# Output projection split, its SSD half between the last GLA heads; layer 1's modulation as running sums on VectorE

## The chip, the core and the metric

The kernel runs on one core of one Trainium2 chip. Its time is device microseconds of one execution, from the first instruction to the end. TensorE (PE) multiplies, VectorE (DVE), ScalarE (ACT) and GpSimd (POOL) work elementwise, SyncE (SP) issues most of the DMAs. Every engine takes its own instructions in order. The order in which the instructions of an engine stand in its queue is laid down at compile time, by a planner that goes by the order of the program, by an estimate of every instruction's duration and by when buffers come free. So an instruction written earlier can stand later in the queue.

## What is computed

Two layers of a diffusion backbone over 256 latent tokens and 256 context tokens (512 columns in all, context first), width 1024. Each layer has a mixer and a squared-ReLU MLP, and every sub-layer is modulated by shift, scale and gate, which come from a matrix product with the conditioning vector (two streams: c for the latents, c_ctx for the context).

```python
for layer in range(DEPTH):
    need_ctx = layer < DEPTH - 1
    mod_l = (silu(c) @ ada_w[layer] + ada_b[layer])[:, None, :]
    mod_c = (silu(c_ctx) @ ada_w[layer] + ada_b[layer])[None, None, :]
    sh1l, sc1l, g1l, sh2l, sc2l, g2l = split(mod_l, 6)
    hl = modulate(rmsnorm(x, norm1_w[layer]), sh1l, sc1l)
    # layer 0: SSD heads || GLA heads;  layer 1: HGRN2 heads || S5 groups
    ol, oc = mixer(hl, hc, ...)          # concat([y, o]) @ w_out
    x = x + g1l * ol
    x = x + g2l * sq_relu_mlp(modulate(rmsnorm(x, norm2_w[layer]), sh2l, sc2l), w1, w2)
    if need_ctx:                         # the same for the context, layer 0 only
        ...
return rmsnorm(x, final_norm_w)
```

In layer 0 the output projection takes 2048 inputs, 1024 of the SSD heads (y) and 1024 of the GLA heads (o). In layer 1 the context's stream needs shift and scale of the first norm alone, since nothing of it is used after that mixer.

## The kernel before

**Products.** Activations lie with features on the 128 partitions and the 512 tokens along the free dimension. A product in float32 is made of three matmuls (`mm3`, all recorded at line 99): each operand is split into a rounded high half and the rest, and high x high, high x low and low x high are added up in PSUM. `wtile` (line 214 issues its DMA on SP's queue) loads 512 KB of weights, a raw tile of 128x1024; ACT copies it to the high half (`whi`, line 80) and DVE subtracts to get the low half (`wlo`, line 87). Raw tiles have four buffers (`RAW`), high and low halves four each (`HL`). A tile of one output block is 8 k-tiles x 3 = 24 matmuls of 512 columns.

**Modulation.** `ada_steps` works out one third of a layer's modulation, a group of 2048 of the 6144 columns. A step loads two raw tiles of 512 KB from ada_w (line 233, SP's queue, from the same four raw buffers) and multiplies them in PE (line 237) with `cs`, 32 columns of which two hold the conditioning of the two streams: four matmuls of 512 columns, each into its own 32 partitions of one PSUM tile. The trace records each as two, so a step has eight records. Eight such steps, then a copy on ACT, then four transposes and the bias: ten steps in all. `ad` runs groups 1 and 2 of layer 0 (group 1 holds gate 1 and shift 2); `step(ad, n)` takes n of its steps. Group (0, 1) is steps 1 to 10 and group (0, 2) is 11 to 20.

**The GLA heads.** Four pairs of heads, `t_` = 0 to 3. `gla_in(t_)` projects q and k out of `h` (tiles hhi and hlo), two output tiles of 24 matmuls, makes the gates and runs a chain of elementwise work between DVE and ACT (`lin_elem`) with short PE pieces (`lin_states`). `gla_out(t_)` makes the attention of both heads with matmuls of 64 and 128 columns, masks on DVE, and scales the result into `vtm`. The loop is a pipeline: the projections of the next pair are written ahead of `gla_out` of this one. `fill` is other work put between: `z_proj`, four groups of 256 columns (96 matmuls of 256 columns each) that gate the SSD result in `xtm`, and a fifth step that norms it. `ZN` says how many of its steps stand before each pair, `ADN` how many modulation steps.

**The output projection** comes after the last pair. It turns xtm (the SSD result, token on partition) with transposes into the two halves of a matmul operand, in the buffers hhi and hlo that h had; loads the residual stream `xT` (2 MB, ACT's queue, into the buffer of xtm, which has to have been read); and makes eight output tiles of the SSD half, each added into xT by `add_out` on DVE with gate 1. Then the GLA half: vtm is turned, four tiles with a modulation step before each, and the last four tiles by halves of the tokens, between which the next norm begins.

**The MLP of layer 0** multiplies 64 weight tiles. `up(k)` makes one hidden block and squares its ReLU (`relu2`: ACT, DVE, ACT, DVE); a second-layer tile is added into xT by `add_out` on DVE. After each of them `step(extra)` takes one step of `background()`, which goes to and fro between `s5_setup` (tables for layer 1, mostly POOL and small DVE instructions) and the modulation of layer 1, groups (1, 0), (1, 1) and (1, 2), 30 steps in all.

Of the kernel before, what the change touches and what calls it, by code (L numbers as in the profile page):

```python
# [10 lines left out]
F32R = mybir.dt.float32r  # L11
# [18 lines left out]
DTM = 11  # L30
NF = 4
AR = 12
ZN = 3, 1, 2, 2
ADN = 0, 6, 11, 0
WA = 0, 1
QP = -2, 1, 2, 5
VP = -2, -1, 0, -1
GP = -1, 0, 4, 6
# [3 lines left out]
def emit(tc, A, out):  # L42
# [43 lines left out]
    def tt(eng, o, a, b, op):  # L86
        eng.tensor_tensor(out=o, in0=a, in1=b, op=op)  # L87
# [7 lines left out]
    def stt(eng, o, a, s, b, op0, op1):  # L95
        eng.scalar_tensor_tensor(out=o, in0=a, scalar=s, in1=b, op0=op0, op1=op1)  # L96
# [47 lines left out]
    cs = tl(cp, [P, 8, 32], "cs")  # L144
    mod = [tl(cp, [P, 48, 2], f"mod{l}") for l in range(2)]
    dskip = tl(cp, [P, 16], "dskip")
    dtb = tl(cp, [64, 1], "dtb")
    nega = tl(cp, [64, 1], "nega")

# [77 lines left out]
    def ada_steps(l, g3, scratch):  # L227
        ps = ps_s()
        for k in range(8):
            raws = [tl(wp, [P, 1024], "wraw", bufs=RAW) for _ in range(2)]  # L230
            for hf in range(2):
                c0 = g3 * 2048 + 1024 * hf
                Q.dma_start(out=raws[hf], in_=A["ada_w"][l, k * P:(k + 1) * P, c0:c0 + 1024])

            last = None
            for gg in (3, 2, 1, 0):
                ins = PE.matmul(ps[32 * gg:32 * gg + 32], lhsT=cs[:, k], rhs=raws[gg // 2][:, gg % 2 * T:gg % 2 * T + T],  # L237
                                start=(k == 0), stop=(k == 7), skip_group_check=True, tile_position=(0, 32 * gg))
                if last is not None:
                    behind(ins, last)  # L240
                last = ins
            yield
        sb = scratch()
        act(sb, ps, AF.Copy)
        yield
        p2 = ps_s()
        for b in range(4):
            tr(p2[:, b * P:(b + 1) * P], sb[:, b * P:(b + 1) * P])
        src = p2.rearrange("p (b g r) -> p g b r", b=4, r=32)[:, :, :, 0:2]
        bias = vA[:, l * 48 + g3 * 16:l * 48 + g3 * 16 + 16].rearrange("p (g b) -> p g b", g=4)  # L250
        dst = mod[l][:, g3 * 16:g3 * 16 + 16].rearrange("p (g b) s -> p g b s", g=4)
        for s in range(2):
            tt(V, dst[:, :, :, s], src[:, :, :, s], bias, ADD)
        yield

    def ada_all(scratch, *lg):
# [3 lines left out]
    def step(it, n=1):  # L260
        for _ in range(n):
            next(it, None)

    def drain(it):
        for _ in it:
            pass
# [998 lines left out]
    def gla_w(t_):  # L1265
        return [wtile(W0, 0, 8, c0 + P * t_, P) for c0 in (3104, 3616)]

    def gla_in(t_, ws):
        qk = []
        for w, sc in zip(ws, (0.125, 1.0)):  # L1270
            ps = ps_d()
            gemm_f(ps, w, ktiles(h))
            d_ = tl(g2, [P, T], "gq" if sc != 1.0 else "gk", bufs=QB)
            act(d_, ps, AF.Copy, scale=sc)
            qk.append(d_)

        def chain(d):
            ps = ps_s()
            b0 = 64 + 32 * d
            mm(ps, gw[b0:b0 + 16, t_ * P:(t_ + 1) * P], dlr[b0:b0 + 16])  # L1280
            gb = vB[:, 24 + 4 * d + t_:25 + 4 * d + t_]
            e1 = tl(g2, [P, T], "ge1", bufs=2)
            act(e1, ps, AF.Abs, bias=gb)
            yield
            act(e1, e1, AF.Exp, scale=-1.0)
            yield
            act(e1, e1, AF.Ln, bias=1.0)
            lg = tl(g2, [P, T], "gc", bufs=2)
            ts(V, lg, ps, gb, ADD, 0.0, MIN)
            yield  # L1290
            tt(V, lg, lg, e1, SUB)
            yield
            nm = f"g{d}"
            qt, kt, kd, el, em = yield from lin_elem(g2, d, lg, qk[0], qk[1], None, 1.0 / 16.0, 0, nm)
            sts = yield from lin_states(g2, d, kd, el, em, lambda c, hh: vtm[:, c, (2 * t_ + hh) * P:(2 * t_ + hh + 1) * P],
                                        2, 0, nm)
            return qt, kt, sts

        return both([chain(d) for d in range(2)])
# [25 lines left out]
            lin_out(g2, pmask, units, put)  # L1325

    scr[0] = lambda: tl(g2, [P, T], "ge1", bufs=2)
    cur = gla_in(0, gla_w(0))
    wn = gla_w(1)
    for t_ in range(4):  # L1330
        step(fill, ZN[t_])
        nxt = gla_in(t_ + 1, wn) if t_ < 3 else None
        wn = gla_w(t_ + 2) if t_ < 2 else None
        step(ad, ADN[t_])
        if t_ == 3:
            drain(fill)
            step(ad, max(0, 10 - adn[0]))
        gla_out(t_, cur)
        cur = nxt
    gla.close()  # L1340


    lo_eng[:] = [V]
    WO = A["ssd_gla_w_out"][0]
    mgs = ExitStack()
    mg = pool("mixg", stack=mgs, side="right")
    scr[0] = lambda: tl(mg, [P, T], "adasb")
    for part, src in enumerate((xtm, vtm)):
        if part == 0:
            mx = [tl(hp, [P, 8, T], n, F32R) for n in ("hhi", "hlo")]  # L1350
        else:
            mx = [tl(mg, [P, 8, T], n, F32R) for n in ("mgh", "mgl")]
        for f in range(8):
            ps = ps_s()
            for c in range(4):
                tr(ps[:, c * P:(c + 1) * P], src[:, c, f * P:(f + 1) * P])
            nw = vB[:, 16 + f:17 + f] if part == 0 else vB[:, 96:97]
            act(mx[0][:, f], ps, AF.Copy, scale=nw)
            stt(V, mx[1][:, f], ps, nw, mx[0][:, f], MUL, SUB)
        if part == 0:  # L1360
            xT = tl(xp, [P, 8, T], "xtm")
            S.dma_start(out=xT, in_=xd.rearrange("k p t -> p k t"))
        def add_out(m):
            def put(s, ps):
                a = HALF[s]
                stt(V, xT[:, m, a], ps[:, a], mod[0][:, 16 + m, s:s + 1], xT[:, m, a], MUL, ADD)
            return put

        nf = 8 if part == 0 else 4
        for m in range(nf):  # L1370
            step(ad, WA[part])
            w = wtile(WO, 8 * part, 8, m * P, P)
            ps = ps_d()
            gemm_f(ps, w, ktiles(mx))
            for s in (1, 0):
                add_out(m)(s, ps)
    drain(ad)
    np_ = ExitStack()
    n1 = pool("norm", stack=np_)
# [64 lines left out]
    s5i = s5_setup(s5s, "right", G)  # L1444

    def background():
        ad = ada_all(lambda: tl(mp, [P, T], "mr", bufs=2), (1, 0), (1, 1), (1, 2))
        for i in range(30):
            step(s5i)
            yield  # L1450
            step(ad)
            yield

        for _ in s5i:
            yield
        s5s.close()
# [266 lines left out]
```

## Time and profile before

| | us |
|---|---|
| three runs | 1475.62, 1479.78, 1483.78; median 1479.78 |
| profiled execution | 1482.16, its span 1480.4 |
| PE busy in the span | 1426.6 (96%) |
| DVE, ACT, POOL busy | 942.2, 688.3, 303.0 |
| GLA heads and the first half of the output projection | from some 285 to 534 |
| MLP of layer 0 | from some 590 to 957 |

The rows below are of one profiled execution; times are microseconds from the start of the span. "Busy" counts the time in which an engine has an instruction in work. The granted clock is 1.00 for 2.4 GHz and 0.50 for 1.2 GHz. A chain of work is followed back from the last instruction to what released each one.

### The profile page before, as it was taken

What the parts mean: (1) busy time and instruction counts of PE and PEld (TensorE: products, weight loads), DVE (VectorE), ACT (ScalarE), POOL (GpSimd) and SP (SyncE); (2) the same over time, 40 slices, a digit from 0 to 9 for tenths busy, and PEclk for the clock granted to TensorE, in tenths of its full rate; (3) what the DMA queues carried; (4) which work ended last, traced back from release to release, by engine and by line L of the source; (5) the groups of instructions that cost most, each with busy time, mean ns of one, the idle gap of its engine ahead of it and who ended that gap; (6) DMA issues with size and microseconds to landing.
All of it is one profiled execution on the core that took longest, in us unless ns stands there. A gap on an engine that the chain in (4) does not pass through costs nothing.

```text
span 1480.4 us, 24457 instructions
## 1 busy us (share of the span) xinstructions
PE 1426.6 (96%) x9662; PEld 1222.3 (83%) x9662; DVE 942.2 (64%) x1596; ACT 688.3 (46%) x1316; POOL 303.0 (20%) x340
## 2 busy tenths in 40 slices
PE   6999999999979999999999999999999999899998
PEld 4788998878746889877777777799988888899998
DVE  4698678876753455854563743374886988655543
ACT  5565545375532234531322422353286786555532
POOL 3000000000000003098077861122500000044210
PEclk9999999999985999999999999999999999999999
DMA  9733444421275433466467656649835332566762
GB/s 333 185 92 85 126 122 118 125 58 58 86 240 160 138 103 105 121 179 197 143 187 218 192 169 186 192 165 202 194 114 157 103 106 66 157 186 170 206 179 86
DMA packets 291151, 222.45 MB, mean 150 GB/s; under 512 B 22902, under 2 KB 270124, under 8 KB 291036
## 3 DMA queue, kind: packets, MB, share of 16 engines
q1 hardware_dynamic: 252752, 182.75, 42.5%
q0 software_dynamic: 6144, 22.05, 4.9%
q10 hardware_dynamic: 32140, 16.09, 4.4%
q8 instruction: 76, 1.25, 0.4%
q14 instruction: 39, 0.32, 0.1%
HBM read 206.39 MB, written 14.46 MB: 149 GB/s over the span
## 4 chain that ended last, share of the span: by engine, by line
PE 78%; DVE 8%; DMA 8%; ACT 4%; issue 2%; ACTq 0%; SPq 0%; DVEq 0%
PE psd L99 65%; PE pss L99 6%; DMA R<-acd 3%; PE pss L237 3%; PE pss L107 2%; DMA araw<-in_ada_w_dram 2%; DVE wlo L87 1%; DMA wraw<-in_ada_w_dram 1%; ACT hL L80 1%; DVE xtm L87 1%; ACT whi L80 1%; PE pss L652 1%; DMA U<-ud 0%; DMA ud<-s5r 0%; ACT R L80 0%
## 5 line engine op out<-in xcount | busy, mean ns | idle before, releaser
L87 DVE TENSOR_TENSOR wlo<-wraw,whi 128x1024 fp32r<-128x1024 f32 (+1 forms) x250 | 323.6, 1298 | 206.7 <-ACT whi L80 205.0
L80 ACT ACTIVATE whi<-wraw 128x1024 fp32r<-128x1024 f32 (+1 forms) x250 | 260.6, 1045 | 351.7 <-DMA wraw<-in_mlp_w_dram 170.7
L99 PE MATMUL psd<-hlo,whi 128*128 128x512 f32 (+1 forms) x1112 | 381.6, 345 | 1.3 <-DVE hlo L87 1.3
L99 PE MATMUL psd<-hhi,whi 128*128 128x512 f32 (+1 forms) x1112 | 378.5, 348 | 3.6 <-ACT hhi L80 3.6
L99 PE MATMUL psd<-hhi,wlo 128*128 128x512 f32 (+1 forms) x1112 | 380.8, 344 | 0.6 <-DVE wlo L87 0.6
L99 PEld LDWEIGHTS psd<-hhi,whi 128*128 128x128 f32 x1112 | 209.5, 191 | 36.0 <-ACT hhi L80 4.2
L99 PEld LDWEIGHTS psd<-hlo,whi 128*128 128x128 f32 x1112 | 211.3, 190 | 25.2 <-DVE hlo L87 2.3
L99 PEld LDWEIGHTS psd<-hhi,wlo 128*128 128x128 f32 x1112 | 211.3, 190 | 25.1 <-DVE wlo L87 1.0
L99 PE MATMUL psd<-wlo,hhi 128*128 128x256 f32 x576 | 165.5, 288 | 2.8 <-DVE wlo L87 2.8
L99 PE MATMUL psd<-whi,hlo 128*128 128x256 f32 x576 | 164.8, 286 | 0.0
L99 PE MATMUL psd<-whi,hhi 128*128 128x256 f32 x576 | 164.4, 287 | 0.0
L99 PEld LDWEIGHTS psd<-wlo,hhi 128*128 128x128 f32 x576 | 111.1, 193 | 4.7 <-DVE wlo L87 3.0
L99 PEld LDWEIGHTS psd<-whi,hhi 128*128 128x128 f32 x576 | 110.8, 193 | 2.7 <-issue 1.3
L99 PEld LDWEIGHTS psd<-whi,hlo 128*128 128x128 f32 x576 | 111.1, 193 | 0.6 <-issue 0.2
L99 PE MATMUL psd<-hidh,whi 128*128 128x512 f32 (+1 forms) x288 | 107.7, 375 | 0.0
L99 PE MATMUL psd<-hidl,whi 128*128 128x512 f32 (+1 forms) x288 | 105.6, 367 | 0.0
L99 PE MATMUL psd<-hidh,wlo 128*128 128x512 f32 (+1 forms) x288 | 105.5, 366 | 0.0
L87 POOL TENSOR_TENSOR nsa<-nsa,nsq 128x256 f32<-128x256 f32 x28 | 26.1, 934 | 370.1 <-ACT nsq L80 369.8
L96 DVE SCALAR_TENSOR_TENSOR xtm<-psd,mod,xtm 128x256 f32<-128x256 f32 x96 | 42.2, 476 | 66.6 <-PE psd L99 59.2
L99 PE MATMUL psd<-hl,whi 128*128 128x256 f32 x256 | 72.9, 285 | 0.0
L99 PE MATMUL psd<-hh,wlo 128*128 128x256 f32 x256 | 72.9, 285 | 0.0
L99 PE MATMUL psd<-hh,whi 128*128 128x256 f32 x256 | 72.4, 283 | 0.0
(448 smaller groups left out, 2447.4 us busy)
## 6 DMA issues: line engine op xcount, KB each, us to landing
wraw<-in_mlp_w_dram SPq DMA_DIRECT2D x128, 512.0 KB, 4.2
wraw<-in_ada_w_dram SPq DMA_DIRECT2D x80, 512.0 KB, 3.8
wraw<-in_ssd_gla_w_in_dram SPq DMA_DIRECT2D x48, 512.0 KB, 4.2
wraw<-in_hgrn_s_w_in_dram SPq DMA_DIRECT2D x43, 512.0 KB, 4.2
araw<-in_ada_w_dram SPq DMA_DIRECT2D x32, 256.0 KB, 7.8
R<-acd ACTq DMA_DIRECT2D x32, 256.0 KB, 3.9
wraw<-in_ssd_gla_w_out_dram SPq DMA_DIRECT2D x16, 512.0 KB, 4.6
wraw<-in_hgrn_s_w_out_dram SPq DMA_DIRECT2D x12, 384.0 KB, 3.4
```

Of the source, the lines that this page charges most:

```text
L80: ins = S.activation(out=out_, in_=in_, func=func, scale=scale, bias=bias)
L87: eng.tensor_tensor(out=o, in0=a, in1=b, op=op)
L96: eng.scalar_tensor_tensor(out=o, in0=a, scalar=s, in1=b, op0=op0, op1=op1)
L99: PE.matmul(o, lhsT=l, rhs=r, start=start, stop=stop, skip_group_check=True)
L107: PE.transpose(o, i, ident[:rows, :rows])
L237: ins = PE.matmul(ps[32 * gg:32 * gg + 32], lhsT=cs[:, k], rhs=raws[gg // 2][:, gg % 2 * T:gg % 2 * T + T], start=(k == 0), stop=(k == 7), ...
L652: PE.matmul(ps[64 * t2:64 * t2 + 64, 64 * a:64 * a + 64], lhsT=W1[i][:, a0 + a, 64 * t2:64 * t2 + 64], rhs=U[:, 2 * (a0 + a) + t2], start= ...
```

## The change

Two parts that don't touch each other.

In the GLA heads, `ZN` and `ADN` are smaller, z is finished before `gla_out(2)`, and the SSD half of the output projection becomes a generator, `ssd_out`. Its first step turns xtm and issues the reload of xT; each further step takes one modulation step and makes one output tile. `SN` takes five steps of it behind `gla_out(2)` and four behind `gla_out(3)`. Modulation steps 11 to 18, which had stood among the heads (11 to 17) and in the GLA half of the output projection, stand before the eight tiles; the two left stand in the GLA half. What the tiles do and their number are unchanged.

In the MLP, layer 1's modulation is no longer multiplied on PE. `ada_sums` takes a group in two halves of 1024 columns. For every k it loads one raw tile and adds it, times the conditioning value of its partition, onto a running sum of 128x1024 on DVE, one sum for each stream: two for group 0, one (the latents') for groups 1 and 2. After eight k the partitions of the sum are added up by PE, with `unit`, 32 columns of which one is 1: four matmuls of 256 columns a stream. The transposes and the bias follow as before. `mod[1]` is set to zero first, for the entries that are no longer computed. The number of steps (ten a group) and of DMAs (16 a group) is the same.

```diff
-ZN = 3, 1, 2, 2
-ADN = 0, 6, 11, 0
-WA = 0, 1
+ZN = 2, 1, 1, 1
+ADN = 0, 6, 4, 0
+SN = 0, 0, 5, 4
...
+    unit = tl(cp, [P, 2, 32], "unit")
+    V.memset(unit, 0.0)
+    for s in range(2):
+        V.memset(unit[:, s, s:s + 1], 1.0)
...
+    def ada_sums(l, g3, scratch, both_):
+        sb = scratch()
+        src_s = (0, 1) if both_ else (0,)
+        for hf in range(2):
+            c0 = g3 * 2048 + 1024 * hf
+            accs = [tl(mp, [P, 1024], f"ada{s}") for s in src_s]
+            for k in range(8):
+                raw = tl(wp, [P, 1024], "wraw", bufs=RAW)
+                Q.dma_start(out=raw, in_=A["ada_w"][l, k * P:(k + 1) * P, c0:c0 + 1024])
+                for s in src_s:
+                    if k == 0:
+                        ts(V, accs[s], raw, cs[:, k, s:s + 1], MUL)
+                    else:
+                        stt(V, accs[s], raw, cs[:, k, s:s + 1], accs[s], MUL, ADD)
+                if k % 2:
+                    yield
+            ps = ps_s()
+            for s in src_s:
+                for g in range(4):
+                    PE.matmul(ps[32 * g:32 * g + 32, :256], lhsT=unit[:, s], rhs=accs[s][:, 256 * g:256 * g + 256],
+                              start=(s == 0), stop=(s == src_s[-1]), skip_group_check=True, tile_position=(0, 32 * g))
+            act(sb[:, 256 * hf:256 * hf + 256], ps[:, :256], AF.Copy)
+        yield
+        p2 = ps_s()
+        for b in range(4):
+            tr(p2[:, b * P:(b + 1) * P], sb[:, b * P:(b + 1) * P])
...
-    for part, src in enumerate((xtm, vtm)):
...
-        nf = 8 if part == 0 else 4
-        for m in range(nf):
-            step(ad, WA[part])
...
+    def ssd_out():
+        mx = [tl(hp, [P, 8, T], n, F32R) for n in ("hhi", "hlo")]
+        turned_mix(mx, xtm, 0)
+        res["x"] = tl(xp, [P, 8, T], "xtm")
+        S.dma_start(out=res["x"], in_=xd.rearrange("k p t -> p k t"))
+        yield
+        for m in range(8):
+            step(ad)
+            out_tile(mx, 0, m)
+            yield
+
     cur = gla_in(0, gla_w(0))
     wn = gla_w(1)
+    so = ssd_out()
     for t_ in range(4):
         step(fill, ZN[t_])
         nxt = gla_in(t_ + 1, wn) if t_ < 3 else None
         wn = gla_w(t_ + 2) if t_ < 2 else None
         step(ad, ADN[t_])
-        if t_ == 3:
+        if t_ == 2:
             drain(fill)
-            step(ad, max(0, 10 - adn[0]))
+            step(ad, 10 - adn[0])
         gla_out(t_, cur)
+        step(so, SN[t_])
         cur = nxt
     gla.close()
...
+    mx = [tl(mg, [P, 8, T], n, F32R) for n in ("mgh", "mgl")]
+    turned_mix(mx, vtm, 1)
+    xT = res["x"]
+    for m in range(4):
+        step(ad)
+        out_tile(mx, 1, m)
     drain(ad)
...
     def background():
-        ad = ada_all(lambda: tl(mp, [P, T], "mr", bufs=2), (1, 0), (1, 1), (1, 2))
+        V.memset(mod[1], 0.0)
+        ad = (x_ for g3 in range(3) for x_ in ada_sums(1, g3, lambda: tl(mp, [P, T], "mr", bufs=2), g3 == 0))
```

## Rows read from the trace of the kernel before

**Rows 1.** The page: busy time by engine; the granted clock in 40 slices.

```profile
PE 1426.6 (96%) x9662; PEld 1222.3 (83%) x9662; DVE 942.2 (64%) x1596; ACT 688.3 (46%) x1316; POOL 303.0 (20%) x340
...
PEclk9999999999985999999999999999999999999999
```

**Rows 2.** Busy time by engine, granted clock and DMA, by stage.

```profile
core 0: us, PE busy (x) PEld busy (x) DVE busy (x) ACT busy (x) POOL busy (x), PEclk, DMA share, GB/s
...
395.00:440.50 45.50, 35.67 (x314) 19.02 (x312) 29.18 (x52) 19.40 (x59) 0.00 (x0) 0.92 0.68 228
440.50:488.50 48.00, 48.00 (x215) 31.47 (x208) 18.05 (x26) 11.81 (x46) 0.00 (x0) 0.50 0.52 157
...
590.00:631.00 41.00, 41.00 (x257) 35.91 (x259) 36.11 (x146) 20.71 (x33) 1.34 (x6) 1.00 0.43 117
631.00:704.00 73.00, 73.00 (x343) 54.51 (x339) 35.87 (x53) 18.30 (x22) 62.53 (x94) 1.00 0.64 191
704.00:740.00 36.00, 36.00 (x169) 28.45 (x162) 17.83 (x26) 13.99 (x20) 0.00 (x0) 1.00 0.49 147
740.00:820.00 80.00, 80.00 (x409) 60.11 (x408) 39.91 (x40) 20.38 (x27) 60.55 (x50) 1.00 0.70 205
820.00:862.00 42.00, 42.00 (x225) 33.27 (x224) 34.36 (x25) 17.41 (x25) 33.52 (x27) 1.00 0.58 174
862.00:957.00 95.00, 95.00 (x484) 71.16 (x483) 35.53 (x50) 25.07 (x32) 20.76 (x22) 1.00 0.61 180
```

**Rows 3.** PE's groups, 395 to 440.5: busy, mean ns, idle before, releaser.

```profile
L237 PE MATMUL pss<-wraw,cs 128*32 128x512 f32 x88 | 12.7, 660 | 8.2 <-DMA wraw<-in_ada_w_dram 8.2
```

**Rows 4.** Busy time in the slice 485 to 490, columns as in rows 2.

```profile
485.00:490.00 5.00, 5.00 (x21) 4.21 (x21) 2.19 (x4) 2.92 (x12) 0.00 (x0) 0.67 0.12 37
```

**Rows 5.** The chain in the MLP: start us, us, what.

```profile
643.04 1.00 PE pss L237 x8
644.03 11.11 PE psd L99 x48
655.14 0.99 PE pss L237 x8
```

**Rows 6.** DMA issues from 395 to 488: KB each, median us to landing.

```profile
wraw<-in_ada_w_dram SPq DMA_DIRECT2D x26, 512.0 KB, 5.3
wraw<-in_ssd_gla_w_out_dram SPq DMA_DIRECT2D x8, 512.0 KB, 4.2
```

**Rows 7.** The page's costliest groups: ACT's copy to the high half.

```profile
L80 ACT ACTIVATE whi<-wraw 128x1024 fp32r<-128x1024 f32 (+1 forms) x250 | 260.6, 1045 | 351.7 <-DMA wraw<-in_mlp_w_dram 170.7
```

**Rows 8.** DVE in order of time: start us, us, what, idle before.

```profile
649.25 1.23 DVE L87 TENSOR_TENSOR wlo<-wraw,whi 128x1024 fp32r<-128x1024 f32 x1 [3.41 <-ACT whi L80]
...
855.57 3.63 DVE L87 TENSOR_TENSOR wlo<-wraw,whi 128x1024 fp32r<-128x1024 f32 x1
```

**Rows 9.** Groups of DVE's instructions from 488.5 to 534, columns as in rows 3.

```profile
L96 DVE SCALAR_TENSOR_TENSOR xtm<-psd,mod,xtm 128x256 f32<-128x256 f32 x15 | 6.5, 479 | 19.6 <-PE psd L99 12.4 <-DMA xtm<-xd 7.3
```

**Rows 10.** Line 237 from 590 to 957: ns min, median, max, first, last start.

```profile
L237 PE MATMUL pss<-wraw,cs x192: 592/605/617, 593.6 to 953.0; 128*32 128x512 f32 x192
```

**Rows 11.** PE in order of time: start us, us, what.

```profile
23.74 0.82 PE L790 MATMUL pss<-araw,cs 128*32 128x256 f32 x8
...
484.84 2.05 PE L99 MATMUL psd<-hhi,whi 128*128 128x512 f32 x4
```

**Rows 12.** Groups of DVE's instructions from 0 to 30, shapes kept apart.

```profile
L91 DVE TENSOR_SCALAR xn<-xt,ss 128x1024 f32<-128x1024 f32 x4 | 2.8, 750 | 8.2 <-ACT ss L80 8.2
```

**Rows 13.** Line 96, columns as in rows 10.

```profile
L96 DVE SCALAR_TENSOR_TENSOR dtu<-dtu,dtl x1: 676/676/676, 148.9 to 148.9; 64x512 f32<-64x512 f32 x1
```

**Rows 14.** Groups of DVE's instructions from 560 to 970, shapes kept apart.

```profile
L87 DVE TENSOR_TENSOR wlo<-wraw,whi 128x1024 fp32r<-128x1024 f32 x66 | 99.0, 1505 | 112.8 <-ACT whi L80 112.7
```

**Rows 15.** Line 237 from 395 to 475, columns as in rows 10.

```profile
L237 PE MATMUL pss<-wraw,cs x120: 592/617/1061, 398.6 to 468.9; 128*32 128x512 f32 x120
```

**Rows 16.** Tile gk, the projected k of a pair, columns as in rows 10.

```profile
L80 ACT ACTIVATE gk<-psd x4: 577/595/597, 290.7 to 395.7; 128x512 f32<-128x512 f32 x4
```

More of the change, by code (lines that the diff above doesn't have):

```diff
@@ L253, in ada_steps @@
             tt(V, dst[:, :, :, s], src[:, :, :, s], bias, ADD)
+        yield
[25 more added lines that the diff above has]
+            tr(p2[:, b * P:(b + 1) * P], sb[:, b * P:(b + 1) * P])
+        for hf in range(2):
+            o_ = g3 * 16 + 8 * hf
+            src = p2[:, 256 * hf:256 * hf + 256].rearrange("p (b g r) -> p g b r", b=2, r=32)
+            bias = vA[:, l * 48 + o_:l * 48 + o_ + 8].rearrange("p (g b) -> p g b", g=4)
+            dst = mod[l][:, o_:o_ + 8].rearrange("p (g b) s -> p g b s", g=4)
+            for s in src_s:
+                tt(V, dst[:, :, :, s], src[:, :, :, s], bias, ADD)
         yield
@@ L1327, in emit, with turned_mix @@
     scr[0] = lambda: tl(g2, [P, T], "ge1", bufs=2)
[L1328 to L1334, printed above, removed]
-        if t_ == 3:
-            drain(fill)
-            step(ad, max(0, 10 - adn[0]))
[L1338 to L1343, printed above, removed]
-    WO = A["ssd_gla_w_out"][0]
-    mgs = ExitStack()
-    mg = pool("mixg", stack=mgs, side="right")
-    scr[0] = lambda: tl(mg, [P, T], "adasb")
-    for part, src in enumerate((xtm, vtm)):
[L1349 to L1352, printed above, removed]
+    WO = A["ssd_gla_w_out"][0]
+    res = {}
+    def turned_mix(mx, src, part):
         for f in range(8):
@@ L1359, in emit, with add_out, put, out_tile @@
             stt(V, mx[1][:, f], ps, nw, mx[0][:, f], MUL, SUB)
[L1360 to L1367, printed above, removed]
-        nf = 8 if part == 0 else 4
-        for m in range(nf):
-            step(ad, WA[part])
[L1372 to L1376, printed above, removed]
+    def add_out(m):
+        def put(s, ps):
+            a = HALF[s]
+            x_ = res["x"][:, m, a]
+            stt(V, x_, ps[:, a], mod[0][:, 16 + m, s:s + 1], x_, MUL, ADD)
+        return put
+    def out_tile(mx, part, m):
+        w = wtile(WO, 8 * part, 8, m * P, P)
+        ps = ps_d()
+        gemm_f(ps, w, ktiles(mx))
+        for s in (1, 0):
+            add_out(m)(s, ps)
+    def ssd_out():
[7 more added lines that the diff above has]
+            out_tile(mx, 0, m)
+            yield
+    cur = gla_in(0, gla_w(0))
+    wn = gla_w(1)
+    so = ssd_out()
+    for t_ in range(4):
+        step(fill, ZN[t_])
+        nxt = gla_in(t_ + 1, wn) if t_ < 3 else None
+        wn = gla_w(t_ + 2) if t_ < 2 else None
+        step(ad, ADN[t_])
+        if t_ == 2:
+            drain(fill)
+            step(ad, 10 - adn[0])
+        gla_out(t_, cur)
+        step(so, SN[t_])
+        cur = nxt
+    gla.close()
+    lo_eng[:] = [V]
+    mgs = ExitStack()
+    mg = pool("mixg", stack=mgs, side="right")
+    scr[0] = lambda: tl(mg, [P, T], "adasb")
+    mx = [tl(mg, [P, 8, T], n, F32R) for n in ("mgh", "mgl")]
[4 more added lines that the diff above has]
+        out_tile(mx, 1, m)
     drain(ad)
```

## The prediction

> **What bounds the kernel now.** I read the page's busy lines and clock strip first, then busy time by stage, then the PE groups, waits and chain of the stages that the change touches. TensorE (PE) is busy 96% of the span, at full clock but for a few slices; the dip that matters lies in the twelfth and thirteenth of the 40 [rows 1]. By stage there are two pictures [rows 2].
>
> The end of the GLA heads (395 to 488.5): from 395 to 440.5 PE works 35.7 of 45.5 us, so it stands idle 9.8 us, 8.2 of them at the modulation matmuls of line 237, waiting for their weights' DMA [rows 3]. From 440.5 to 488.5 it is busy all 48.0 us, but the granted clock is 0.50, the lower level of 1.2 GHz [rows 2]. What runs there are the 64- and 128-column matmuls of the heads and the modulation's. The clock comes back within the slice 485 to 490, in which the 512-column matmuls of the output projection begin [rows 4, 11]. At 2.4 GHz the same 48.0 us would be 24.0. So this end loses some 34 us: 24.0 by the clock, 9.8 by waiting.
>
> The MLP (590 to 957): PE is busy without a gap at full clock, VectorE (DVE) 199.6 of 367 us (36.1 + 35.9 + 17.8 + 39.9 + 34.4 + 35.5) [rows 2]. The chain there is PE and nothing else: two weight tiles of 24 matmuls in 11.11 us, one modulation step in 1.00, two tiles again [rows 5]. Whatever leaves PE here shortens the run, until DVE or the weights end last.
>
> **Part A, the output projection between the heads.** It adds no work. Moved are the eight transposed tiles of the SSD half with their high and low halves, eight output tiles with their weight DMAs (SP's queue), the 2 MB reload of the stream (ACT's queue), eight modulation steps that now stand before those tiles, and one z group, which goes from head pair 1 to 2. An output tile is 24 matmuls of 512 columns, half of 11.11 = 5.6 us [rows 5]; eight are 44 us of 512-column work that need not follow the last head any more.
>
> Clock: if those tiles share the low stretch, up to 24.0 us come back. Turning xtm needs the z projection finished, and hhi/hlo free of the last head's projections, so the first outputs of head pair 2 (some 10 us of PE) will still stand without cover; I take 20, with ends of 24 and 4.
>
> Idle time: the first eight modulation steps keep their places between pairs 1 and 2, now with a z group beside them. I take half of 9.8, so 5, ends 0 and 9.8.
>
> New waits: each of the eight tiles now follows a modulation step, so 1.5 MB go through the four raw buffers in 5.6 + 1.0 = 6.6 us, 227 GB/s; 228 were moved from 395 to 440.5 [rows 2]. But the next tile's weights get their buffer only when PE has done a modulation step, and then need 4.2 us to land [rows 6], 1.05 for the high half [rows 7] and 1.23 for the low half [rows 8]: 6.5 us against 6.6 of cover. That just fits if they have the queue to themselves. Behind another load they take 5.3 to land [rows 6], which is 1.0 us too late, eight times 8 us. The reload is worth up to 7.3: so long did DVE wait for it before [rows 9], and now the last head's elementwise work is queued behind such a wait. Its issue on ACT's queue costs nothing while PE has tiles to do. I take 4, ends 0 and 15.
>
> Sum of A: -20 - 5 + 4 = **-21 us** (ends -24 - 9.8 = -34 and -4 + 15 = +11; -5 if the clock alone is weak, or the other two).
>
> On the clock a row and a rule part. The row: 48.0 of 48.0 us busy at 0.50. The Trainium skill (TensorE: Matmul & The Clock Gate, Part 1: The HAM clock gate) calls the low rate the default that activity releases; the trace shows an engine without a pause that was not released. By that rule of the Trainium skill the stretch would already have run at full rate, and a fuller PE would give nothing back there.
>
> **Part B, layer 1's modulation as running sums.** Removed from PE: 24 modulation steps (192 records of line 237 [rows 10], eight a step), each 1.00 us of the chain [rows 5]: -24.0. Added on PE: per half of a group four 256-column matmuls for each stream, so (2 + 1 + 1) x 2 = 8 sets of four. Half the columns of a step of 1.00 are 0.5 us each; the eight records of a set at the start of the kernel span 0.82 [rows 11]. At 0.5 the sets cost +4, at most +8 with a step's full 1.00. The twelve transposes stay; the ScalarE copies are split in two and hide beside PE.
>
> Added on DVE: 64 instructions of 128x1024. Eight are tensor_scalar, 0.75 us by a row of that shape [rows 12]. 56 are scalar_tensor_tensor, a shape that the trace lacks; at 512 elements that form takes 0.676 [rows 13], so its time goes with the elements as for the low half's subtraction, which at 1024 takes 1.23 in quiet time and 1.505 on average in this stage, because while GpSimd (POOL) runs it is stretched, once to 3.63 [rows 8, 14]. I take 1.5: 56 x 1.5 + 8 x 0.75 = 90 us. DVE goes from 200 to 290 of some 350 us: hidden on average.
>
> Not everywhere. From 631 to 704 both streams are summed: six steps of four sums at 1.5 add 36 to 35.9 on DVE, 72 in a stage that PE could do in 67. From 820 to 862 DVE has 34.4 of 42, and seven sums at 2 us make it 48. What queues behind a late sum is the low half of the next weights, the squares of relu2 and the add_outs; PE is reached when the lead is gone. A low half begun at 649.25 is done at 650.5, and the next pair starts at 656.1, so the lead is some 5 us [rows 5, 8]. Against that the sums give their raw buffers back without waiting for PE, and weights can come earlier. I take +4, ends 0 and +13 (5 + 8).
>
> Sum of B: -24 + 4 + 4 = **-16 us** (ends -24 + 4 = -20, and -24 + 8 + 13 = -3).
>
> **Total.** The profiled execution took 1482.2 us (span 1480.4), 2.4 above the median of 1479.8. 1482.2 - 21 - 16 = 1445.2; less 2.4, **1443**.
>
> **The rivals.**
> 1. *The tiles don't land between the heads, or the clock does not follow.* The planner sets the queue order by its own estimate of what is ready: six modulation steps are written between head pairs 1 and 2, yet none ran before 398.6, when the projections of pair 3 were already done, their last copied out at 395.7 [rows 15, 16]. Tiles that stay behind the last head, or heads that still run alone at 0.50, leave A at 0 to -5: 1482.2 - 16 - 5 - 2.4 = 1459, up to 1464. Against it: the clock rose where 512-column matmuls came in. The rule of the Trainium skill (TensorE: Matmul & The Clock Gate, Part 1) ends here too, since it leaves the clock nothing to follow; the trace does not agree with it at 440.5.
> 2. *DVE ends last in the MLP.* With +13 of waits and +8 for the sets B is -3: 1482.2 - 21 - 3 - 2.4 = 1456. For it: the two crowded stretches; against: idle DVE time around them.
> 3. *Everything is hidden:* -34 - 20 - 2.4 gives 1426.
> 4. *Slower: the sums are blocked by GpSimd throughout.* If each took the 3.63 us of the longest row, DVE would need 199.6 + 64 x 3.63 = 432 us for 367 of PE, +65; with A that is 1482.2 + 65 - 21 - 2.4 = 1524. It decides from (367 + 21 + 7.4 - 199.6) / 64 = 3.06 us a sum, where the run would be 0.5% slower. POOL is busy 62.5 of 73 us from 631 to 704 [rows 2]; against it, the average there is 1.505. The Trainium skill (SBUF — State Buffer, Who interferes with whom) speaks against the change: a VectorE instruction with two SBUF inputs and a GpSimd instruction that reads SBUF exclude each other, the later one waiting until the first is done. The stretched rows agree.
> 5. *Neither part pays:* a weak clock (-4), the idle time as it was and +4 of waits make A 0, and B is -3: 1477, no change to speak of.
>
> **How the numbers follow.** 0.5% of 1480 is 7.4 us, about what a measurement tells from no change. Forecast 0.48; rival 1: 0.19; rival 2: 0.12; rival 3: 0.09; rival 5: 0.06; rival 4: 0.06. The range holds the forecast and rivals 1 to 3 with a few us for the baseline (its three runs span 8.2): 1421 to 1468, 0.82 or so. Faster is the forecast and rivals 1 to 3, 0.88; same is rival 5, 0.06; slower rival 4, 0.06.
>
> **What would show it.** Right for A: the 48 us at 0.50 gone or cut to about 10, output tiles of the SSD half standing among the heads' matmuls, the start of the MLP some 21 us earlier. Wrong: the same low stretch, or PE idle for w_out weights or the reload. Right for B: no line-237 matmuls in the MLP, weight tiles back to back, the stage some 16 us shorter with DVE near 290 busy. Wrong: PE idle before psd matmuls, released by low halves or by relu2, above all in the two crowded stretches. A start of the MLP that is no earlier, or a stage no shorter, makes the prediction wrong by the part's whole sum.

## The result and the profile after

The changed kernel took **1489.59 us** (median of 11 executions, 1485.55 to 1501.43); the kernel before, run beside it, 1477.62 (11 executions, 1460.64 to 1487.61). The ratio is 1.0127, 95% interval 1.0089 to 1.0165 (of the medians 1.008): slower, by about one per cent. The forecast was 1443, faster; the time lies above its whole range.

The profiled execution spans 1486.2 us, 5.8 more than before. Three cuts in both traces split it: the first copy of a projected q, the last matmul of the output projection, the last matmul of layer 0's MLP.

| stage | before, us | after, us | difference | forecast |
|---|---|---|---|---|
| start to first q copy | 290.2 | 284.6 | -5.6 | 0 |
| heads and output projection | 293.4 | 302.1 | +8.7 | -21 |
| MLP | 393.6 | 396.5 | +2.9 | -16 |
| rest | 503.2 | 503.0 | -0.2 | 0 |

The first line is no gain of the change: executions whose start is the same reach that point anywhere from 284.6 to 290.5 us.

The 57 executions of the kernel before that ran beside the experiments fall into two bands of time and of TensorE's granted clock (41 at 1472 to 1484 us, 16 at 1451 to 1465 us), which is itself a finding, below, so each experiment is set against the median of all executions of the kernel before that ran beside it.

The page after, to be held against [rows 1]:

```profile
PE 1414.0 (95%) x9534; PEld 1221.1 (82%) x9534; DVE 1028.9 (69%) x1666; ACT 686.0 (46%) x1319; POOL 332.7 (22%) x340
...
PEclk9999999998597899999999999999999999999999
```

PE is busy for 12.6 us less, where some 20 were forecast, and VectorE (DVE) for 86.7 more, near the 90 forecast. But the dip of the clock strip has not been filled: it stands two slices earlier, and a second, shallower one follows it.

Busy time by stage, after; columns as in [rows 2]:

```profile
345.00:410.00 65.00, 55.99 (x334) 33.73 (x333) 37.27 (x61) 26.58 (x88) 0.00 (x0) 0.68 0.24 82
410.00:458.00 48.00, 42.15 (x280) 34.69 (x279) 24.75 (x38) 16.61 (x41) 0.00 (x0) 0.82 0.30 99
458.00:545.00 87.00, 85.91 (x464) 61.65 (x464) 39.80 (x59) 26.61 (x66) 0.00 (x0) 0.93 0.58 174
...
590.00:631.00 41.00, 39.98 (x254) 35.81 (x254) 39.22 (x100) 18.54 (x30) 1.03 (x1) 1.00 0.53 152
631.00:704.00 73.00, 73.00 (x334) 59.76 (x333) 68.49 (x139) 23.38 (x30) 38.33 (x54) 1.00 0.67 198
704.00:740.00 36.00, 30.73 (x141) 24.38 (x140) 11.79 (x14) 5.70 (x8) 33.78 (x42) 0.91 0.35 117
740.00:820.00 80.00, 72.75 (x349) 58.06 (x348) 64.08 (x61) 21.19 (x29) 57.25 (x41) 0.96 0.58 175
820.00:862.00 42.00, 42.00 (x222) 33.55 (x221) 38.23 (x24) 15.71 (x23) 40.60 (x31) 1.00 0.58 180
862.00:960.00 98.00, 94.23 (x450) 74.91 (x449) 66.91 (x76) 29.87 (x41) 34.77 (x27) 0.98 0.70 208
```

The first three rows of the kernel before in the same cuts:

```profile
345.00:410.00 65.00, 63.34 (x477) 50.33 (x475) 42.96 (x67) 29.46 (x84) 0.00 (x0) 1.00 0.25 81
410.00:458.00 48.00, 39.83 (x251) 20.83 (x250) 24.59 (x41) 16.35 (x57) 0.00 (x0) 0.75 0.61 205
458.00:545.00 87.00, 87.00 (x412) 67.35 (x409) 40.67 (x58) 28.06 (x59) 0.00 (x0) 0.83 0.48 145
```

**The heads.** From 458 on SSD tiles stand among the last heads' matmuls, and the clock is 0.93 instead of 0.83. That the tiles did this isn't shown: a_only, with the same order, has 0.88 there, and one execution of the kernel before (before_x2, below) 0.96. The loss is ahead of that. From 345 to 410 PE was at full clock and nearly full; now it is at 0.68 and idle for 9.0 us. The z tiles that stood among the outputs of the first heads now run at 409 to 427, and those outputs, the modulation steps and the gates are left alone. Over 345 to 545 PE's idle time went from 9.8 to 15.9 us, and the time at the low clock from the first q copy to the last output matmul from 58.0 to 71.7 us. PE's groups from 350 to 410 show what the idle time waits for:

```profile
L241 PE MATMUL pss<-wraw,cs 128*32 128x512 f32 x48 | 9.8, 922 | 2.3 <-DMA wraw<-in_ada_w_dram 2.3
...
L107 PE MATMUL pss<-ident,ke 128*128 128x128 f32 x6 | 1.8, 440 | 6.7 <-DVE ke L87 6.7
```

The modulation's matmuls (line 241 now, 237 before) take 922 ns in the mean, and the turn of ke waits 6.7 us for DVE: a chain from engine to engine that the z tiles had covered.

**The MLP.** PE was busy without a gap in [rows 2]; now it is idle for 17.3 of 370 us (370 less 352.7), 12.5 of them from 704 to 820. From 704 to 740 DVE, too, does only 11.8 us of work. What PE waits for from 590 to 960 (us in total, times, longest), and the same for DVE:

```profile
PE psd L99 <- DVE wlo L87: 8.0, 4, 4.2
PE pss L107 <- ACT mr L80: 5.3, 1, 5.3
PE pss L640 <- POOL cl L87: 3.0, 1, 3.0
```

```profile
DVE blk L592 <- POOL cma L87: 16.4, 1, 16.4
...
DVE ada L96 <- DMA wraw<-in_ada_w_dram: 12.3, 8, 4.8
```

DVE in order of time, after (start us, us, what, idle before):

```profile
709.99 0.70 DVE L592 MEMSET blk<- 128x768 f32 x1
727.13 0.70 DVE L592 MEMSET blk<- 128x768 f32 x1 [16.45 <-POOL cma L87]
727.75 0.63 DVE L87 TENSOR_TENSOR hidl<-mr,hidh 128x512 fp32r<-128x512 f32 x1
728.29 0.99 DVE L91 TENSOR_SCALAR ada<-wraw,cs 128x1024 f32<-128x1024 f32 x1
729.21 1.61 DVE L87 TENSOR_TENSOR wlo<-wraw,whi 128x1024 fp32r<-128x1024 f32 x1
```

A 0.70 us memset of the S5 setup takes 17.1 us of the queue. Its tile, blk, is taken from the memory that a table of GpSimd (POOL), ph, held, so it must wait until POOL has made that table and the transfer that takes it out (`phd<-ph`) has landed. The profile names POOL's cma, which ended at the same moment. But in the kernel before, the change, b_only and b_mid alike the memset starts 0.28 us after this landing (in the change 727.13 after 726.85), and in two of them the profile names the transfer; in the kernel before this wait was 5.5 us. Behind the memset stand the relu2's low half and the next weights' low half, and PE runs dry. PE's longest gap, 5.3 us, comes by way of ScalarE, which waits for that low half, with the copy of the modulation's sums next in its queue (start us, us, what, idle before):

```profile
728.47 0.60 ACT L80 ACTIVATE mr<-psd 128x512 f32<-128x512 f32 x1 [15.80 <-DVE hidl L87]
728.96 0.38 ACT L80 ACTIVATE mr<-pss 128x256 f32<-128x256 f32 x1
```

POOL is late because its first operation of this setup began at 662.9 us, 76 us after the output projection's end, where it began at 629.4, 46 us after it, in the kernel before: the small DVE operations that lead up to it stand among the 32 sums of group 0 (in b_mid and b_one, below, with 16 sums there, it begins 59 and 58 us after). Four dips of the clock, 17.1 us in all, come with PE's gaps; before there was none in the MLP.

The sums themselves cost what was forecast (ns min, median, max):

```profile
L96 DVE SCALAR_TENSOR_TENSOR ada<-wraw,cs,ada x56: 1270/1285/3474, 607.6 to 945.2; 128x1024 f32<-128x1024 f32 x56
L91 DVE TENSOR_SCALAR ada<-wraw,cs x8: 746/751/1660, 606.2 to 926.2; 128x1024 f32<-128x1024 f32 x8
```

### The profile page after: what moved, and what is told of

The parts are those of the page before. It is cut to its first block, busy times and chain, and to the rows that moved or that the text cites. A ratio compares the mean times of both kernels' runs of the same rounds, so it can differ in the third digit from the quotient of the medians.

```text
span 1486.2 us, 24320 instructions
## 1 busy us (share of the span) xinstructions
PE 1414.0 (95%) x9534; PEld 1221.1 (82%) x9534; DVE 1028.9 (69%) x1666; ACT 686.0 (46%) x1319; POOL 332.7 (22%) x340
## 4 chain that ended last, share of the span: by engine, by line
PE 63%; DVE 14%; DMA 10%; POOL 5%; ACT 4%; issue 4%; SPq 0%; ACTq 0%; DVEq 0%; POOLq 0%
PE psd L99 53%; PE pss L99 6%; DVE wlo L87 4%; DMA R<-acd 3%; DMA wraw<-in_ada_w_dram 2%; POOL cmb L87 2%; PE pss L107 2%; POOL cma L87 2%; DMA araw<-in_ada_w_dram 2%; DVE ada L96 1%; DMA wraw<-in_ssd_gla_w_out_dram 1%; PE pss L241 1%; ACT whi L80 1%; DVE mr L87 1%; ACT hL L80 1%
## 5 line engine op out<-in xcount | busy, mean ns | idle before, releaser
L99 PE MATMUL psd<-hhi,whi 128*128 128x512 f32 (+1 forms) x1112 | 382.9, 349 | 3.7 <-ACT hhi L80 3.6
L96 DVE SCALAR_TENSOR_TENSOR ada<-wraw,cs,ada 128x1024 f32<-128x1024 f32 x56 | 88.4, 1590 | 12.5 <-DMA wraw<-in_ada_w_dram 12.3
```

The lines of the kernel that those rows point to most:

```text
L99: PE.matmul(o, lhsT=l, rhs=r, start=start, stop=stop, skip_group_check=True)
```

## The experiments

In all of them "stage A" is from the first q copy to the last output matmul and "MLP" from there to the MLP's last matmul, both in the one profiled execution; "low" is the time at the lower clock in stage A; the ratio is between medians. Each expectation names its theories for itself.

| kernel | ratio | stage A, us | low, us | MLP, us |
|---|---|---|---|---|
| before | | 293.4 | 58.0 | 393.6 |
| after | 1.008 | 302.1 | 71.7 | 396.5 |
| a_only | 1.007 | 306.7 | 81.9 | 394.0 |
| a_oldz | 0.998 | 287.5 | 41.0 | 394.1 |
| a_early | 1.002 | 298.9 | 47.8 | 394.1 |
| a_m1 | 0.994 | 286.9 | 30.7 | 394.7 |
| a_m1newz | 1.005 | 301.7 | 71.7 | 394.2 |
| b_only | 1.004 | 294.2 | 61.4 | 396.4 |
| b_none | 0.977 | 294.5 | 61.4 | 364.6 |
| b_blkG | 0.995 | 293.8 | 58.0 | 385.1 |
| b_mid | 1.005 | 297.9 | 68.3 | 401.0 |
| b_one | 0.992 | 294.1 | 61.4 | 376.3 |
| ab_best | 0.992 | 295.4 | 64.9 | 386.5 |

### The two parts alone

a_only is the change with `ada_all` put back in `background`; b_only is the kernel before with `ada_sums` there.

> The first part of the change alone: the SSD half of the output projection split, with the new ZN, ADN and SN; layer 1's modulation stays on TensorE as before. Theory P (the planner's place): the change's profile took 301.9 us from the first copied q to the last output-projection matmul against 293.2 before, so this part costs some 9 us: 1.006 of before, between 1.003 and 1.010. Rival Q (the two parts only hurt together, as one shifts the clock or the DMAs for the other): this part alone gives back the 21 us forecast, 0.986.

> The second part of the change alone: running sums on VectorE in the MLP, the GLA stage as before. Theory S (VectorE's queue): the MLP keeps what the change's profile shows, from the last output-projection matmul to the last MLP matmul 396.6 us against 393.8, so 1.000 to 1.005 of before, with the same wait of VectorE for GpSimd before the memset of blk, near 16 us. Rival Q (only together): the 16 us forecast come, 0.989.

Measured: a_only 1489.13 us, b_only 1484.98, the kernel before beside them 1479.16. (One of the six executions of a_only took 7097 us and is not explained; the median without it is 1487.82.) Each part is slower by itself, and each in its own stage: a_only's MLP and b_only's stage A are those of the kernel before within 0.8 us. So they can be taken apart separately.

### Part A: the z tiles back at their places

```diff
-ZN = 2, 1, 1, 1
+ZN = 3, 1, 2, 2
```

> As a_only, but with ZN as before the change (3, 1, 2, 2), so that the z groups stand where they stood. Theory P: the z group again covers the first pair's outputs, and only the last two pairs' outputs run alone; the stage is 5 to 12 us shorter than in a_only, 0.997 to 1.002 of before. Rival R (the loss of part A comes from the output tiles and their buffers, not from the moved z group): as a_only, 1.006.

a_oldz differs from a_only by this line alone: 1475.76 us against 1489.13, stage A 287.5 against 306.7, so 19.2 us shorter, more than the theory's 5 to 12. The stretch from 345 to 410 in a_only, then in a_oldz:

```profile
345.00:410.00 65.00, 56.53 (x335) 34.50 (x334) 37.27 (x61) 26.48 (x88) 0.00 (x0) 0.67 0.25 82
```

```profile
345.00:410.00 65.00, 63.37 (x479) 49.41 (x477) 43.04 (x66) 30.71 (x94) 0.00 (x0) 1.00 0.22 74
```

The moved z group is what part A lost by: clock and idle time are back at once.

### Part A: the tiles ahead of the heads' outputs

a_early, on top of a_oldz, writes the SSD steps ahead of the heads' outputs in both turns; a_m1 only in the third, with the last four steps behind the last head:

```diff
 a_early:
+        step(so, SN[t_])
         gla_out(t_, cur)
-        step(so, SN[t_])
 a_m1:
-SN = 0, 0, 5, 4
+SN = 0, 0, 0, 4
+SB = 0, 0, 5, 0
+        step(so, SB[t_])
         gla_out(t_, cur)
         step(so, SN[t_])
```

> As a_oldz, but the steps of the SSD output projection are written ahead of the outputs of pairs 2 and 3 and not behind them; in the planned queue of TensorE seven of the eight output tiles then stand among the outputs of the last two pairs, where in the change it is one, and two more between the last ones. Theory P: the 48 us at half clock before the output projection shrink below 15 us, the stage is 12 to 25 us shorter than before, 0.983 to 0.992. Rival R (waits for weights through the four raw buffers and for the reload eat what the clock gives back): 0.997 to 1.005, with TensorE idle or VectorE waiting for DMAs in that stage.

> Part A alone with the z tiles at their old places; the turn and four SSD tiles are written ahead of the third head's outputs, the other four behind the last head's, so that the planned queue has tiles among the outputs of both heads and some left for the time in which the GLA half is turned. Theory P (every matmul of the heads that stands beside an output tile runs at full clock, and what a_early lost was the uncovered end of the last head, 13 us of low clock and 6.7 us of idle TensorE at 510-545): scan to last output matmul 280-286 us, time at the low clock under 30 us there, the whole at 0.988-0.995 of the kernel before. Rival R (the low clock moves to the next uncovered place, whatever is covered): 290 us or more, over 40 us at the low clock, the whole at 0.997-1.004.

a_early: 1481.89 us, no gain. The ratio is rival R's, but not for R's reason: the tiles then cover the third head, nothing is left for the end of the last, and there PE waits for DVE and not for weights, with the clock low for 17.1 us from 522.6 on. From 458 to 545, and PE's waits from 500 to 545:

```profile
458.00:545.00 87.00, 79.81 (x397) 57.16 (x397) 34.63 (x51) 22.07 (x59) 0.00 (x0) 0.86 0.45 137
```

```profile
PE pss L99 <- DVE vtm L87: 4.6, 1, 4.6
PE pss L107 <- DVE vtm L87: 2.0, 1, 2.0
```

a_m1 keeps four for it: 1470.98 against 1480.32, stage A 286.9, low 30.7, each a little past the bound of its expectation. a_m1newz is a_m1 with the change's ZN:

> a_m1 with the change's ZN (z tiles 2, 1, 1, 1 and the rest at the third turn), nothing else. Theory Z (the z tiles were the cover of the first heads' outputs; taken away there they leave small matmuls at half clock between 350 and 410 us): scan to last output matmul 297-303 us against 286.9, time at the low clock 45-60 us against 30.7, the whole at 1.000-1.007 of the kernel before. Rival (the place of z matters only with the change's own order of the tiles): 290 us or less, 0.991-0.996.

1484.11 against 1476.62, stage A 301.7. From 345 to 410 in a_m1newz:

```profile
345.00:410.00 65.00, 56.46 (x333) 35.53 (x331) 34.88 (x57) 24.95 (x79) 0.00 (x0) 0.66 0.26 89
```

In two orders of the tiles the place of z is worth 15 to 19 us of the stage and 13 of the median. It is not the chance of one execution either: in all three profiles with the change's ZN (after, a_only, a_m1newz) the clock is low for 44 to 51 us between 359 and 418, and in none of the 14 others is it low anywhere from 312 to 401. That is settled.

### Part B: what the steps were worth, and the wait

All three start from b_only. b_none drops both the steps and the sums; b_blkG fills blk on POOL; b_mid sums the groups in the order 1, 0, 2:

```diff
 b_none:
+        ad = iter(())
 b_blkG:
-            V.memset(blk[i], 0.0)
+            G.memset(blk[i], 0.0)
-                V.tensor_copy(blk[i][...], BB[i][...])
+                G.tensor_copy(blk[i][...], BB[i][...])
 b_mid:
-        ad = (x_ for g3 in range(3) for x_ in ada_sums(...))
+        ad = (x_ for g3 in (1, 0, 2) for x_ in ada_sums(...))
```

> The kernel before without any of layer 1's modulation: neither the TensorE steps nor the running sums, so layer 1's shift, scale and gate are left out (zero). It measures the first term of part B by itself. Theory S (the steps' TensorE time stands on the path of the MLP, worth 24 us, and what the change gave back came after that): the MLP from the last output matmul to its last product falls from 393.6 us to 368-372 us, the whole to 0.982-0.986 of the kernel before. Rival (other limits of the MLP hide most of it, so the steps were never worth 24 us): 385 us or more, the whole at 0.995 or more.

> Part B alone, with the two memsets and four copies that fill blk given to GpSimd instead of VectorE, so that the 16.4 us wait for GpSimd's tables no longer stands at the head of VectorE's queue. Theory H (that one wait in an in-order queue starves TensorE of low halves and costs most of what the steps gave): the MLP falls from 396.4 us to 380-386 us, the whole to 0.989-0.995 of the kernel before. Rival C (VectorE is crowded over the whole stretch, the wait only stood where it would have been late anyway): the MLP 393 us or more, the whole at 1.001-1.006.

> Part B alone, with the groups in the order 1, 0, 2: group 1 (16 sums, one stream) comes first and group 0 (32 sums, both streams) in the middle, where VectorE was idle for half of the time. The work is the same. Theory C (the 32 sums of the first group fill VectorE between 600 and 700 us, so that the small operations of the S5 setup wait behind them and GpSimd's chain starts late): the wait of the memset of blk falls from 16.4 us to under 6 us, the MLP from 396.4 us to 382-388 us, the whole to 0.991-0.996 of the kernel before. Rival H (a wait at a fixed place of the queue, whatever runs before it): wait over 12 us, MLP 393 us or more, the whole at 1.001-1.006.

b_none: the MLP is 29.0 us shorter than in the kernel before, a little more than the theory's 22 to 26. Twelve transposes, 1.8 us of PE, go with the steps. The steps' time was on the path in full.

b_blkG: 1472.30 against 1480.32, MLP 385.1, both as theory H said. Its row for the worst stretch, and PE's waits from 590 to 960:

```profile
704.00:740.00 36.00, 36.00 (x175) 29.07 (x174) 26.74 (x25) 10.31 (x15) 34.40 (x35) 1.00 0.62 196
```

```profile
PE pss L107 <- POOL wt L87: 6.8, 2, 5.2
PE psd L99 <- DVE wlo L87: 1.9, 1, 1.9
```

POOL's setup starts as late as in the change (655.6 us, 76 us after the output projection), so nothing became earlier. Only the place of the wait changed: POOL waits for itself, and DVE goes on. That gives 11 us of the MLP, with the 3.8 us of memsets and copies that DVE no longer does. Of what PE still waits for, 6.8 of 8.7 us is POOL's late setup (`wt`), and not DVE.

b_mid: 1488.03, MLP 401.0. Theory C had the reason for POOL's late start right, but not the gain. Time and MLP lie where rival H put them, though the wait, 11.4 us, is under H's 12 and did depend on what ran before it. POOL started earlier (59 us after the output projection), the memset still waited for the table's transfer, and the 32 sums of group 0 fill DVE further on: 70.1 of 80 us from 740 to 820, where PE is idle for 9.9. DVE's waits from 590 to 960, then PE's longest:

```profile
DVE ada L96 <- DMA wraw<-in_ada_w_dram: 19.2, 9, 3.8
...
DVE blk L592 <- DMA phd<-ph: 11.4, 1, 11.4
```

```profile
PE psd L99 <- DVE wlo L87: 14.1, 6, 6.2
```

Spreading the sums differently moves the loss and doesn't remove it. b_one is b_blkG without the context's sums (`False` in place of `g3 == 0`):

> b_blkG without the sums of the context's stream in group 0: 48 sums instead of 64 and six sets of unit matmuls instead of eight; the context's shift and scale of layer 1 are left out (zero). With blk out of the way the MLP took 385.1 us, against 364.6 us without any modulation: 20.5 us are still paid for the sums. Theory V (VectorE's time as such, each sum the same): a quarter of it goes, MLP 378-381 us. Theory G (only the double stretch of group 0, 32 sums in a row, delays TensorE): most of it goes, MLP 368-375 us. Rival (it is the raw tiles' transfers and GpSimd, not the number of sums): 384 us or more.

MLP 376.3, between the two theories: 8.8 of the 20.5 us that b_blkG had over b_none go with a quarter of the sums. PE's waits from 590 to 960:

```profile
PE psd L99 <- DVE wlo L87: 2.2, 3, 1.2
PE psd L99 <- DVE xtm L96: 1.0, 1, 1.0
```

So the gain isn't a price for each sum. POOL's setup begins 58 us after the output projection instead of 76, PE no longer waits for POOL (6.8 us in b_blkG), and the low clock in the MLP falls from 10.2 to 3.4 us. The 20.5 us of b_blkG can be added up from its profile: 4.7 of unit matmuls, 1.8 of transposes, 8.7 of idle PE and 5.1 for the clock (half of 10.2) make 20.3. Of b_one's 11.7, 3.8 of unit matmuls, 1.8, 3.2 and 1.7 make 10.5, more than half of it work of PE itself. What DVE's waits for the raw tiles of the sums cost (12.3 us in the change, 14.2 in b_one) no run separates.

### Both mends, and the clock

ab_best is the change with ZN, SN and SB of a_m1 and blk on POOL.

> The change with three mends: the z tiles at their old places, the turn and four SSD tiles ahead of the third head's outputs (as in a_m1), and blk filled by GpSimd (as in b_blkG). If the two parts stand in different stages and add up: scan to last output matmul 285-290 us, MLP 384-387 us, the whole 15 us under the kernel before, 0.986-0.992 of it. Rival (the parts meet: what one frees the other takes, or the clock finds other low stretches): one of the two stages above 290 or 390 us, the whole at 0.993 or more.

1465.07 against 1476.62, the fastest version that keeps the whole computation, with the MLP as expected; stage A of its profile was 295.4 all the same. Its profile was the slowest of its twelve executions, at 1473.75 us. For that, and for the two bands of the kernel before, the same kernels were profiled in further executions:

> The kernel before, another execution. Theory M (the bands differ by the low stretch near 440-488 us): an execution at 1472-1484 us has 50-65 us at the low clock between the first gq copy and the last output matmul and that stage takes 290-298 us; one at 1451-1466 us has under 30 us there and 272-283 us. Rival (the bands come from another stage, the start or the transfers): the stage within 291-296 us in both bands.

> As the run before it: theory M wants time, low clock and length of the stage to go together (1472-1484 us: 50-65 us low, 290-298 us; 1451-1466 us: under 30 us low, 272-283 us); the rival wants the stage at 291-296 us whatever the time.

> As the two runs before it, for one more execution: theory M 290-298 us of the stage with 50-65 us low at 1472-1484 us, or 272-283 us with under 30 us low at 1451-1466 us; the rival 291-296 us in either case.

> The kernel of ab_best, another execution. Its first profile was the slowest of its twelve executions (1473.75 us, granted clock 0.967, low for 44 us from 401 us on; the median was 1465.07 us at 0.978). If that stretch belongs to the execution: scan to last output matmul 284-289 us with 25-45 us at the low clock, the whole at 1460-1468 us, the MLP 384-388 us as before. If it belongs to the order of work: again 293-297 us with over 55 us low, the whole at 1470-1475 us.

| execution | time, us | stage A, us | low, us | MLP, us |
|---|---|---|---|---|
| before_x1 | 1480.79 | 294.0 | 58.0 | 393.6 |
| before_x2 | 1463.19 | 276.5 | 17.1 | 394.2 |
| before_x3 | 1478.45 | 294.6 | 64.9 | 394.2 |
| ab_best_x | 1461.63 | 283.3 | 27.3 | 386.3 |

In these profiles the difference between the bands lies in stage A and in its low stretch. Below is the kernel before, first in the profile that the forecast read, then in before_x2: the 26 us from 440 on, before any output tile (the first comes at 484.8 and at 466.5), and one group of matmuls of the heads, which both have run by 488.

```profile
440.00:466.00 26.00, 26.00 (x120) 15.18 (x120) 7.36 (x13) 3.31 (x20) 0.00 (x0) 0.51 0.41 135
...
L99 PE MATMUL pss<-vtm,pa 128*128 128x128 f32 x32 | 12.5, 495 | 0.0
```

```profile
440.00:466.00 26.00, 24.92 (x189) 16.43 (x184) 16.67 (x24) 9.44 (x35) 0.00 (x0) 0.95 0.91 258
...
L99 PE MATMUL pss<-vtm,pa 128*128 128x128 f32 x32 | 8.4, 348 | 0.9 <-DVE pa L87 0.9
```

The program and its order are the same. The heads alone, without a single tile for cover, ran at 0.51 in the first and at 0.95 in before_x2. What decides between the two no row shows: from 395 to 440 both are at 0.92 with 35.2 and 35.8 us of PE, and in all four executions of the kernel before PE is idle for 1.0 to 1.5 us, waiting for a modulation weight, shortly before 440 (the gap ends between 437.4 and 440.0). In three the clock falls within 0.7 us after this gap, in before_x2 it does not. It stays open.

Across these 57 executions of the kernel before, time goes with the mean granted clock at 12.3 us for each 0.01 (correlation -0.98). Set on such lines at the same clock of 0.972, the kernel before takes 1480.9 us, a_m1 1483.9, b_blkG 1470.3 and ab_best 1470.9 (each worked out from its own executions; a_m1's begin at 0.974, the others have this clock inside their range). So b_blkG's gain is there at a given clock. a_m1's is all in the clock that it gets, 0.984 in the median. ab_best is faster than the usual execution of the kernel before. But neither it nor a_m1 (1465.07 and 1470.98 us) is faster than the faster band of the kernel before, whose median is 1462.3.

## Why the prediction was wrong, point by point

**The bottleneck** was read rightly. The MLP is TensorE's: b_none makes it 29.0 us shorter where the removed steps were put at 24.0 (1.8 us of transposes are in the 29.0 too).

**Part A, clock: -20.** Measured: 13.7 us more at the low clock, worth some 6.9 (half of it). The step that failed here is "Moved are ... and one z group", which was listed and given no price. The z tiles were the cover of the first heads, so their move left a low clock for 44.4 of the 51 us from 361 to 412; taking it back is worth 15 to 19 us. The rest of the term was over-sized: with the z tiles back (a_oldz) the stage is 5.9 us below the profile of before, with tiles among both heads too (a_m1, ab_best_x) 6.5 to 10.1, not 21. And the 24.0 us were read from one execution, with three times at hand that all lay in the slower band: before_x2 doesn't lose them, nor, by their times, do 16 of the 57. A loss that more than one execution in four doesn't have should have entered at a part of its size, with a wider range. By the rule of the Trainium skill (TensorE: Matmul & The Clock Gate, Part 1: The HAM clock gate) activity releases the low rate. From 440 to 466 before_x2 agrees at 0.95; the other three executions of the kernel before, with PE busy for all 26.0 us, do not: they stayed at 0.50 to 0.51.

**Part A, idle: -5.** Measured +6.1 from 345 to 545 (9.8 to 15.9 us), +3.3 over the whole stage. The waits for the modulation's weights shrank from 8.2 to 2.3 us, as hoped, and the dependency of ke on DVE took 6.7, uncovered by the same move.

**Part A, new waits: +4.** Less came of it: from 458 to 545 PE was idle for 1.1 us. So the bound of +15 from late weights was not reached. A's +8.7 lies within the ends given for it (-34 to +11), but that is luck, since the +11 stood on late weights; and the range of the whole left this end out.

**Part B, removed -24, added sets +4.** Right: 27.2 without the transposes, and the unit matmuls cover 4.7 us of PE:

```profile
590.00:960.00 370.00, 4.70 (x64) 1.47 (x64) 0.98 0.60 181
```

**Part B, sums at 1.5 us, DVE at 290.** Right: 1.59 in the mean, and 288.7 us busy from 590 to 960. Rival 4, sums blocked throughout, did not come: they took 1.27 at the least and 3.47 at the most. The 26 sums with no POOL instruction beside them took 1.29 at the most, the other 30 took 1.86 in the mean. Here the rule of the Trainium skill (SBUF — State Buffer, Who interferes with whom) and the trace agree, at that size.

**Part B, late sums: +4 (0 to +13).** This is the second step that failed. It counted how much work DVE has in a stretch and how long a low half could be late. It did not follow the S5 setup, whose small DVE operations release POOL and whose memset waits for POOL: the sums delayed these operations, POOL began 30 us later, and that came back to DVE as one wait of 16.4 us at the head of its queue. From b_none the sum is 364.6 + 4.7 (unit matmuls) + 1.8 (transposes) + 17.3 (PE idle) + 8.6 (half of 17.1 at the low clock) = 397.0, against 396.5 us measured: so idle time and clock cost 25.9 us where +4 stood. Taking the wait off DVE's queue is worth 11 of that (b_blkG). Most of the idle time that is left then is PE's own wait for the late POOL, 6.8 us, and it goes when the sums of the context's stream are left out (b_one).

**The signs said beforehand.** "PE idle before psd matmuls, released by low halves or by relu2" came for 8.0 of the 17.3 us of idle time. But most of this time lay between the two crowded stretches, from 704 to 820, and none in them. For A the sign "the same low stretch" came two slices early.

**The rivals.** Rival 2 named the place, DVE in the MLP, and put B at -3; it was +2.9. Rival 1 named the clock and the tiles' landing and put A at 0 to -5; it was +8.7. Neither could be positive as priced, since neither had a mechanism that takes cover away or lets an engine wait for one that it had itself delayed. The chance for slower stood on GpSimd's blocking alone.

## What to carry to other kernels

When a step moves, price the place it leaves as well as the place it goes to: the large matmuls of z were cover for the clock and for the engine-to-engine chains beside them. When work is added to an in-order engine that is idle "on average", follow every operation of another engine that it releases, and any wait for that engine in its own queue; give such a wait to the engine that it waits for. And before a clock stretch enters a sum, look at it in several executions.

## What the runs showed of the hardware that was not expected

The granted clock of one unchanged instruction order isn't one number. The kernel before gave 0.51 and 0.95 over the same 26 us of its heads in different executions, and its times fell into the two bands named above. The same holds for ab_best: 44.4 us at the low clock from 401 us on in one execution, none longer than 13.7 us in another. In the MLP of the change each of the four dips of the clock, 3.4 or 6.8 us long, comes with a short gap of PE: the first two begin within gaps of 5.3 and 4.2 us, the other two within 0.6 us after gaps of 3.0 and 1.8 us. The gap of 1.8 had one of 1.2 us some 7 us ahead of it. A gap of 1.0 us at 593 has no dip behind it. Of the change's eleven executions none had a mean clock above 0.967.
